# A two-layer attention trunk in fp32: where tables, inputs, gates and fetched outputs have their places, and in which order the last projection runs

## The chip, the cores and the metric

The kernel runs on one core of a Trainium2 chip. The metric is the device time of one execution in microseconds (us); the median over several executions counts. The engines are TensorE (PE in the profile; its weight loads, PEld, run beside its matmuls), VectorE (DVE), ScalarE (ACT), GpSimd (POOL) and SyncE (SP), which issues all DMAs of this kernel. Each engine takes its instructions in order.

## The reference, cut to what matters

The input is x, 2048 tokens by 1024 channels. Two layers follow each other, each with a residual sum:

```python
# layer 0
h = rms_norm(x, norm_g)
aq, ak, av, ag, bq, bk, bv, bg = split(h @ w_in)
aq, ak = rope(rms_norm(aq)), rope(rms_norm(ak))      # 8 query heads, 2 key heads of 64
ya = sliding_window_sink_attention(aq, ak, av, sinks) * silu(ag)
yb = chunked_relbias_attention(rms_norm(bq), rms_norm(bk), bv, rel) * silu(bg)
x = x + concatenate([ya, yb]) @ w_out
# layer 1
h = rms_norm(x, norm_g)
q, k, v, gate = split(h @ w_in)                      # 8 heads of 2 x 64, values of 128
q1, q2, k1, k2 = rope(rms_norm(...))
a = softmax(mask(q1 k1)) - lam * softmax(mask(q2 k2))
o = rms_norm(a @ v, subln_g) * (1 - lambda_init)
x = x + (o * silu(gate)) @ w_out
```

The sink is one more entry of each softmax row, so the row's maximum is also taken with it. Rope needs tables of cos and sin, multiplied by the norm's gains.

## The kernel before

All matmuls of projections and scores are in fp32 accuracy: operands are split into a high and a low part (names ending in H and L, made by a copy on ScalarE and a subtraction on VectorE or GpSimd), and `mm3` (L214 to L216) issues three matmuls for each product.

Tokens are in four blocks of 512. The kernel has four stages: layer 0's projection (names p0, to about 605 us), its attention with output projection (m, to about 1190), layer 1's projection (p1, to 1776) and layer 1's attention with gates and output projection (c, to the end). Layer 0's projection writes queries, keys, values and gates to DRAM, but leaves its last eight gate tiles to the next stage: `late_gate` there computes them between attention heads, on tiles of `yp`'s ring "xr", which has two slots (L783, L784). Layer 0's output tiles (`out_tile`, L495 to L505) take an x tile by DMA, accumulate in PSUM, add (L504) and store.

Layer 0's attention A takes the row maximum of two query tiles at once (L635) and then the minimum with the negated sink (L636, 128x2), which the exponential on ScalarE (L640) needs.

Each projection fetches cos and sin into the ring "xt" of its pool `xp` (three tiles, L267 to L270), which x tiles use too, and `rope_tables` (L185 to L193) builds two pairs of tables on VectorE: eight products of 128x512 and three scalings in each layer. In layer 1 the tables come first in the program. `weights` (L302 to L310) loads two weight tiles per DMA and splits them, the low part on GpSimd; with `first` set, every other low part goes to VectorE. The first two blocks' hidden tiles are then made from x: norm (L324, L326), transposes (L331), high and low part (L335, L336).

Layer 1's attention loops over heads and query blocks: scores (L913, L914), their maximum (L917) and exponential (L920), then transposes (L959) and products with values (L966), a norm by a matmul with ones (L991) and the gate. In blocks but the first the head's output is stored to DRAM, and `fetch` (L1016 to L1021) brings it back as "oy" and splits it at once on ScalarE (L1012) and GpSimd (L1013), for the output projection, which runs between the heads (`projected`, and `projected_last` for the last block: column half 1 in four PSUM tiles at a time, then half 0). "oy", the x tiles and the gates share ring "ot" of four.

Which work stands in which order is settled when the kernel is built: the program yields work in units that `pace` mixes, and a list scheduler with a simulated timeline then orders each engine's instructions; buffers of a ring are taken in program order. The pools of a stage are laid one behind another in the order in which they are opened. The first use of a pool waits for all users of every older pool on whose storage it lies. In layer 1's attention the pool `ld`, which holds queries, is opened third and lies over the projection's weight tiles (`wp`) and x tiles. `issue_after` puts an instruction behind another in its engine's order without a semaphore of its own.

Of the kernel before, what the change touches and what calls it, by code (L numbers as in the profile page):

```python
# [10 lines left out]
F32 = mybir.dt.float32  # L11
# [74 lines left out]
class Trunk:  # L86
# [137 lines left out]
    def _project(self, es, layer):  # L224
# [39 lines left out]
        def tables():  # L264
            if layer == 0:
                self.parameters(xp.tile([P, D], F32, tag="xt", name=n + "tmp"))
            self.cos = xp.tile([P, S // P, 32], F32, tag="xt", name=n + "cos")  # L267
            self.sin = xp.tile([P, S // P, 32], F32, tag="xt", name=n + "sin")
            nc.sync.dma_start(self.cos, a["cos"].rearrange("(t p) d -> p t d", p=P))
            nc.sync.dma_start(self.sin, a["sin"].rearrange("(t p) d -> p t d", p=P))  # L270
            gq, gk = ("ev_a_q_norm", "ev_a_k_norm") if layer == 0 else ("od_q_norm", "od_k_norm")
            tabs["q"] = self.rope_tables(tb, self.gain[gq], 0.125, n + "tq")
            tabs["k"] = self.rope_tables(tb, self.gain[gk], 1.0, n + "tk")
# [145 lines left out]
        for half in range(2):  # L419
# [13 lines left out]
            for gi, (kind, c0, width, o) in enumerate(groups):  # L433
                w = ready or weights(c0, width)
# [54 lines left out]
    def out_tile(self, y, w, j, t, c, xin, xout, sb, pmm, n, tag, xtag="xr", xbufs=None, order=range(KT), after=None):  # L489
# [14 lines left out]
        nc.vector.tensor_tensor(xr, ps, xr, ALU.add)  # L504
# [18 lines left out]
    def _mix0(self, es):  # L523
# [71 lines left out]
        def join(yt, O, e):  # L595
            hi = slice(e * HD, (e + 1) * HD)
            lo = slice((1 - e) * HD, (2 - e) * HD)
            tmp = sb.tile([P, BLK], F32, tag="low", name=n + "low")
            nc.scalar.activation(tmp[hi, :], O[lo, :], AF.Copy)
            nc.vector.tensor_tensor(yt[hi, :], O[hi, :], tmp[hi, :], ALU.add)  # L600
# [14 lines left out]
        def scores_a(h, b, res):  # L615
# [7 lines left out]
            for z in range(2):  # L623
# [12 lines left out]
                nc.vector.tensor_scalar(nm[:, zs], nm[:, zs], self.nsink[:, h:h + 1], None, ALU.min)  # L636
# [117 lines left out]
        def projected(b):  # L754
# [11 lines left out]
            for j, c in units:  # L766
                while next_load(c):
                    pass
                pm, tag = (pO, "O") if b == 0 and j % 2 else (pmm, "om")
                after = follow if b and (j, c) == units[-1] else None  # L770
                yield from self.out_tile(
                    split[b], w, j, b * NTB + j, c, a["x"], self.x1, yp, pm, n, tag, xbufs=2, order=ended, after=after
                )

        def late_gate(b, c, wg, h, r0):
# [7 lines left out]
            sg = yp.tile([P, BLK], F32, tag="xr", name=n + "sg", bufs=2)  # L783
# [73 lines left out]
    def _mix1(self, es):  # L857
        nc, tc, a, s = self.nc, self.tc, self.a, self.s1
        n = "c"
        pool = lambda nm, bufs, **kw: es.enter_context(tc.tile_pool(name=n + nm, bufs=bufs, **kw))  # L860
        ot = pool("ot", 4)
        sm = pool("sm", 8)
        ld = pool("ld", 2)
        yp = pool("y", 2 * KT)
        vp = pool("v", 4)
        pp = pool("pp", 20)
# [25 lines left out]
        def scores(h, b, q, K, res, then):  # L892
# [4 lines left out]
            for j in range(NTB):  # L897
# [9 lines left out]
                for m in range(2):  # L907
                    chunks = []
                    for z, (c, ce) in enumerate(cuts):
# [10 lines left out]
                        nc.scalar.activation(chunks[z][:, :wd], ps, AF.Exp, bias=nm[:, m, z:z + 1], accum_out=acc)  # L920
# [94 lines left out]

        def fetch(h, b):  # L1016

            if (h, b) in ended and h not in y[b]:
                o = ot.tile([P, BLK], F32, tag="ot", name=n + "oy")
                nc.sync.dma_start(o, s["o"][h * P:(h + 1) * P, b * BLK:(b + 1) * BLK])  # L1020
                split(h, b, o)  # L1021
# [53 lines left out]
        def out_begin(b, j, c):  # L1075
# [3 lines left out]
            pl, tag = (pG, "G") if b < NB - 1 else (pS, "S")  # L1079
# [11 lines left out]
        def projected(b):  # L1091
# [3 lines left out]
            for i, c in enumerate(halves):  # L1095
                for j in range(NTB):
                    xr, ps, to = out_begin(b, j, c)
                    for k in range(KT):
                        out_step(b, j, k, ps, w)
                        if j == NTB - 1 and i == 0:  # L1100
                            load_w(halves[1], k, w[k])
                        elif j == NTB - 1:
                            fetch(k, b + 1)
# [4 lines left out]
        def projected_last():  # L1108
# [15 lines left out]
            for c, w in ((1, w[0]), (0, pairs)):  # L1124
                tiles = [out_begin(b, j, c) for j in range(NTB)]
                for k in range(KT):
                    while (k, b) not in ended:
                        yield 0
                    for j in range(NTB):
                        out_step(b, j, k, tiles[j][1], w)  # L1130
                    yield 1
                for t in tiles:
                    out_end(*t)
# [45 lines left out]
        def side():  # L1179
            yield from gates()  # L1180
            for b in range(NB):
                for h in range(8):
                    while (h, b) not in ended and b < NB - 1:
                        yield 0
                    fetch(h, b)
# [50 lines left out]
```

## Time and profile before

| | us |
|---|---|
| median of 3 runs | 2843.03 (2841.9 to 2843.21) |
| the profiled execution | 2843.39 |
| its span in the trace | 2841.6 |
| TensorE busy | 2707.3 (95%) |
| VectorE busy | 1844.8 (65%) |
| GpSimd busy | 1596.6 (56%) |
| ScalarE busy | 1543.8 (54%) |

All rows below are of the profiled execution; their times count from the start of its span. In a timeline a row has start, length, engine, line, operation, result and operands, shape and count, and in brackets the idle time of the engine ahead of it and what ended that. In a table of windows a row has the stretch, its length, the busy time (and number of instructions) of TensorE, its weight loads, VectorE, ScalarE and GpSimd, the clock granted to TensorE as a share of full speed, the DMA engines' busy share and the GB/s moved. Waits are given as total us, number of times and longest.

### The profile page before, as it was taken

Reading aid. Unit: us, or ns where it says so; the run is one execution under the profiler, and the core shown is the slowest. Engines: PE = TensorE matmul, PEld = TensorE weight load, DVE = VectorE, ACT = ScalarE, POOL = GpSimd, SP = SyncE. Lnnn points to the kernel's source line nnn. Section 1 sums busy time; section 2 is a strip of 40 time slices with the busy share of each in tenths; the row PEclk is TensorE's granted clock in tenths of the full one; section 3 lists DMA queues with packets and bytes.
Section 4 is the critical chain, followed back from the end, with each engine's and each line's share of the span. In section 5 each row is a group of like instructions: output and inputs, shape, how many; then the busy total and the mean of one; then the engine's idle time right before and its main releaser. Section 6 shows DMA issues by size and latency. Waiting matters only on the chain.

```text
span 2841.6 us, 43911 instructions
## 1 busy us (share of the span) xinstructions
PE 2707.3 (95%) x13384; PEld 2171.4 (76%) x13384; DVE 1844.8 (65%) x4643; ACT 1543.8 (54%) x4015; POOL 1596.6 (56%) x1740
## 2 busy tenths in 40 slices
PE   7999999999899999899999999899999999999998
PEld 5888888887788888777788888777676777676766
DVE  7752285347788886498808870468787777666651
ACT  4443543367766666243334331468787676666751
POOL 3541252234545454267745560468888887888871
PEclk9999999999999999999999999999999999999999
DMA  5674343738887765476885443887868676464542
GB/s 161 228 233 149 108 140 120 220 117 232 218 197 186 190 181 150 155 271 198 254 255 189 141 126 108 251 251 212 248 187 232 180 212 207 120 191 131 176 137 81
DMA packets 356092, 521.68 MB, mean 184 GB/s; under 512 B 44816, under 2 KB 139792, under 8 KB 355856
## 3 DMA queue, kind: packets, MB, share of 16 engines
q1 hardware_dynamic: 355856, 518.87, 61.6%
q8 instruction: 107, 1.75, 0.3%
q14 instruction: 129, 1.06, 0.1%
HBM read 361.70 MB, written 157.02 MB: 183 GB/s over the span
## 4 chain that ended last, share of the span: by engine, by line
PE 73%; DVE 9%; DMA 9%; ACT 4%; issue 2%; POOL 2%; SPq 1%; DVEq 0%; ACTq 0%; POOLq 0%
PE cO L966 7%; PE p1mm L214 5%; PE p1mm L216 5%; PE p1mm L215 5%; PE cS L913 4%; PE cS L914 4%; PE ctr L959 3%; PE p0mm L214 3%; PE p0mm L216 3%; PE p0mm L215 3%; PE com L214 2%; PE com L215 2%; PE com L216 2%; PE mom L214 2%; PE cG L214 2%
## 5 line engine op out<-in xcount | busy, mean ns | idle before, releaser
L920 ACT ACTIVATE cP<-cS,cnm 128x512 f32<-128x512 f32 (+3 forms) x640 | 397.3, 628 | 181.6 <-DVE cnm L917 142.9
L917 DVE TENSOR_REDUCE cnm<-cS 128x1 f32<-128x512 f32 (+3 forms) x640 | 371.7, 601 | 80.0 <-PE cS L914 74.1
L936 POOL TENSOR_SCALAR cP<-cP,crl,ce 128x512 f32<-128x512 f32 (+3 forms) x288 | 220.0, 778 | 164.2 <-DVE crl L931 84.7
L215 PE MATMUL p1mm<-p1wL,p1hH 128*128 128x512 f32 x768 | 302.3, 394 | 0.4 <-POOL p1wL L310 0.4
L214 PE MATMUL p1mm<-p1wH,p1hH 128*128 128x512 f32 x768 | 301.1, 393 | 0.8 <-ACT p1wH L308 0.8
L216 PE MATMUL p1mm<-p1wH,p1hL 128*128 128x512 f32 x768 | 301.8, 393 | 0.0
L310 POOL TENSOR_TENSOR p0wL<-p0ws,p0wH 128x512 fp32r<-128x512 f32 (+1 forms) x124 | 149.4, 1237 | 266.8 <-ACT p0wH L308 257.8
L966 PE MATMUL cO<-cpt,cv 128*128 128x512 f32 (+3 forms) x640 | 287.7, 537 | 4.2 <-DVE cpt L964 3.6
L946 POOL TENSOR_TENSOR cP<-cP,cP 128x512 f32<-128x512 f32 (+3 forms) x256 | 285.5, 1140 | 1.4
L913 PE MATMUL cS<-ck,cqd 128*128 128x512 f32 (+3 forms) x640 | 261.2, 413 | 12.4 <-ACT cP L920 7.1
L214 PE MATMUL p0mm<-p0wH,p0hH 128*128 128x512 f32 (+1 forms) x640 | 239.9, 377 | 5.2 <-ACT p0vt L472 3.5
L310 POOL TENSOR_TENSOR p1wL<-p1ws,p1wH 128x512 fp32r<-128x512 f32 x128 | 169.2, 1342 | 133.6 <-ACT p1wH L308 126.4
L216 PE MATMUL p0mm<-p0wH,p0hL 128*128 128x512 f32 (+1 forms) x640 | 239.6, 375 | 1.8 <-DVE p0hL L336 1.8
L215 PE MATMUL p0mm<-p0wL,p0hH 128*128 128x512 f32 (+1 forms) x640 | 239.2, 374 | 0.0
L914 PE MATMUL cS<-ck,cql 128*128 128x512 f32 (+3 forms) x640 | 231.4, 367 | 4.4 <-DMA cql<-qL 4.4
L959 PEld LDWEIGHTS ctr<-ident,cP 128*128 128x128 f32 x1088 | 136.8, 141 | 109.7 <-issue 60.8
L945 POOL TENSOR_SCALAR cP<-cP,crl,ce 128x512 f32<-128x512 f32 (+3 forms) x230 | 180.0, 795 | 0.0
L959 PE MATMUL ctr<-ident,cP 128*128 128x128 f32 x1088 | 172.9, 274 | 0.8 <-ACT cpt L962 0.3
L214 PEld LDWEIGHTS p1mm<-p1wH,p1hH 128*128 128x128 f32 x768 | 144.7, 188 | 29.8 <-ACT p1wH L308 1.0
L215 PEld LDWEIGHTS p1mm<-p1wL,p1hH 128*128 128x128 f32 x768 | 144.7, 188 | 29.5 <-POOL p1wL L310 0.8
L216 PEld LDWEIGHTS p1mm<-p1wH,p1hL 128*128 128x128 f32 x768 | 144.7, 188 | 28.8
L913 PEld LDWEIGHTS cS<-ck,cqd 128*128 128x128 f32 x640 | 121.9, 191 | 44.6 <-ACT cP L920 19.9
(306 smaller groups left out, 7271.1 us busy)
## 6 DMA issues: line engine op xcount, KB each, us to landing
p1ws<-in_od_w_in_dram SPq DMA_DIRECT2D x56, 512.0 KB, 4.4
p0ws<-in_ev_w_in_dram SPq DMA_DIRECT2D x48, 512.0 KB, 4.4
ck<-kH SPq DMA_DIRECT2D x144, 128.0 KB, 3.3
ck<-kL SPq DMA_DIRECT2D x144, 128.0 KB, 3.5
cv<-v SPq DMA_DIRECT2D x72, 256.0 KB, 4.5
cqd<-qH SPq DMA_DIRECT2D x128, 128.0 KB, 4.6
cql<-qL SPq DMA_DIRECT2D x128, 128.0 KB, 4.6
cwH<-wgH SPq DMA_DIRECT2D x64, 256.0 KB, 4.6
```

The lines of the kernel that those rows point to most:

```text
L214: mm(ps, aH, bH, start=first, stop=False)
L215: mm(ps, aH, bL, start=False, stop=False)
L216: mm(ps, aL, bH, start=False, stop=last)
L310: low.tensor_tensor(l[:, :width], ws[:, k, :width], f32(h[:, :width]), ALU.subtract)
L913: mm(ps, qd[:, m, js], kt[:, :wd], start=True, stop=False)
L914: self.anchor = mm(ps, ql[:, m, js], kt[:, :wd], start=False, stop=True).ins
L917: nc.vector.tensor_reduce(nm[:, m, z:z + 1], ps, AX.X, ALU.max, negate=True)
L920: nc.scalar.activation(chunks[z][:, :wd], ps, AF.Exp, bias=nm[:, m, z:z + 1], accum_out=acc)
L936: nc.gpsimd.tensor_scalar(p1, p1, rl[:, 0:1], e1, ALU.mult, ALU.mult)
L946: nc.gpsimd.tensor_tensor(p1, p1, p2, ALU.add)
L959: nc.tensor.transpose(tp[:, (j - j0) * P:(j - j0 + 1) * P], us[j][kt // 4][:, kk:kk + P], self.ident)
L966: mm(O[:, j0 * P:], v, T[:, :wd], start=(kt == 0), stop=(kt == nkt - 1), skip_group_check=True)
```

## The change

Seven edits:

1. cos and sin go into ring "xn" of pool `sb` (5 tiles) in both layers, and layer 1's tables are ordered behind the last sum of layer 0 (`self.added`). The first weights of layer 1 take their odd low parts on VectorE (`first`).
2. "low" in layer 0's attention has one buffer instead of two, and "sg" of the late gates a buffer of its own in that pool.
3. The sink minimum is two operations of 128x1.
4. For layer 0's last output block the even x tiles come from pool `yt`.
5. Layer 1's attention opens `ld` first, then `sm` and `ot`; "P0" has 19 buffers instead of 20.
6. Fetched outputs have a ring "oy" of two; their split is issued one fetch later (or ahead of the next projection), behind the newest exponential in ScalarE's order.
7. `projected_last` accumulates half 1 to the last head but one, then one tile of half 0 (`ahead`, in the bank of the gates), then the last head for both, and the other tiles of half 0 one by one.

```diff
--- before.py
+++ after.py
@@ -264,13 +264,14 @@
                 self.parameters(xp.tile([P, D], F32, tag="xt", name=n + "tmp"))
-            self.cos = xp.tile([P, S // P, 32], F32, tag="xt", name=n + "cos")
-            self.sin = xp.tile([P, S // P, 32], F32, tag="xt", name=n + "sin")
+            self.cos = sb.tile([P, S // P, 32], F32, tag="xn", name=n + "cos", bufs=5)
+            self.sin = sb.tile([P, S // P, 32], F32, tag="xn", name=n + "sin", bufs=5)
             nc.sync.dma_start(self.cos, a["cos"].rearrange("(t p) d -> p t d", p=P))
...
             gq, gk = ("ev_a_q_norm", "ev_a_k_norm") if layer == 0 else ("od_q_norm", "od_k_norm")
-            tabs["q"] = self.rope_tables(tb, self.gain[gq], 0.125, n + "tq")
-            tabs["k"] = self.rope_tables(tb, self.gain[gk], 1.0, n + "tk")
+            with self.tc.issue_after(self.added) if layer else nullcontext():
+                tabs["q"] = self.rope_tables(tb, self.gain[gq], 0.125, n + "tq")
+                tabs["k"] = self.rope_tables(tb, self.gain[gk], 1.0, n + "tk")
@@ -431,7 +432,7 @@
             for gi, (kind, c0, width, o) in enumerate(groups):
-                w = ready or weights(c0, width)
+                w = ready or weights(c0, width, first=half == gi == 0)
                 ready = None
@@ -501,7 +502,7 @@
             yield 1
-        nc.vector.tensor_tensor(xr, ps, xr, ALU.add)
+        self.added = nc.vector.tensor_tensor(xr, ps, xr, ALU.add).ins
         nc.sync.dma_start(xout[tok, cs], xr)
@@ -595,7 +596,7 @@
             lo = slice((1 - e) * HD, (2 - e) * HD)
-            tmp = sb.tile([P, BLK], F32, tag="low", name=n + "low")
+            tmp = sb.tile([P, BLK], F32, tag="low", name=n + "low", bufs=1)
             nc.scalar.activation(tmp[hi, :], O[lo, :], AF.Copy)
@@ -633,7 +634,8 @@
                 nc.vector.tensor_reduce(nm[:, zs], ps, AX.X, ALU.max, negate=True)
-                nc.vector.tensor_scalar(nm[:, zs], nm[:, zs], self.nsink[:, h:h + 1], None, ALU.min)
+                for j in (2 * z, 2 * z + 1):
+                    nc.vector.tensor_scalar(nm[:, j:j + 1], nm[:, j:j + 1], self.nsink[:, h:h + 1], None, ALU.min)
                 yield 1
@@ -767,9 +769,10 @@
                 pm, tag = (pO, "O") if b == 0 and j % 2 else (pmm, "om")
+                xp, xt, xb = (yp, "xr", 2) if b or j % 2 else (self.yt, "yt", None)
                 after = follow if b and (j, c) == units[-1] else None
                 yield from self.out_tile(
-                    split[b], w, j, b * NTB + j, c, a["x"], self.x1, yp, pm, n, tag, xbufs=2, order=ended, after=after
+                    split[b], w, j, b * NTB + j, c, a["x"], self.x1, xp, pm, n, tag, xtag=xt, xbufs=xb, order=ended, after=after
                 )
@@ -780,7 +783,7 @@
                 yield 1
-            sg = yp.tile([P, BLK], F32, tag="xr", name=n + "sg", bufs=2)
+            sg = sb.tile([P, BLK], F32, tag="sg", name=n + "sg", bufs=1)
             gt = yp.tile([P, BLK], F32, tag="xr", name=n + "gt", bufs=2)
@@ -858,12 +861,12 @@
         pool = lambda nm, bufs, **kw: es.enter_context(tc.tile_pool(name=n + nm, bufs=bufs, **kw))
+        ld = pool("ld", 2)
+        sm = pool("sm", 8)
         ot = pool("ot", 4)
-        sm = pool("sm", 8)
-        ld = pool("ld", 2)
         yp = pool("y", 2 * KT)
         vp = pool("v", 4)
-        pp = pool("pp", 20)
+        pp = pool("pp", 19)
         kp = pool("kp", 4)
@@ -917,7 +920,9 @@
                         acc = la[:, m, z:z + 1] if nb > 1 else l[:, m:m + 1]
-                        nc.scalar.activation(chunks[z][:, :wd], ps, AF.Exp, bias=nm[:, m, z:z + 1], accum_out=acc)
+                        self.exp = nc.scalar.activation(
+                            chunks[z][:, :wd], ps, AF.Exp, bias=nm[:, m, z:z + 1], accum_out=acc
+                        ).ins
                         then(j, m, z)
@@ -1013,12 +1018,19 @@
+        fetched = []
+
         def fetch(h, b):
...
             if (h, b) in ended and h not in y[b]:
-                o = ot.tile([P, BLK], F32, tag="ot", name=n + "oy")
+                o = ot.tile([P, BLK], F32, tag="oy", name=n + "oy", bufs=2)
                 nc.sync.dma_start(o, s["o"][h * P:(h + 1) * P, b * BLK:(b + 1) * BLK])
-                split(h, b, o)
+                fetched.append((h, b, o))
+
+        def split_fetched(left):
+            if len(fetched) > left:
+                with tc.issue_after(self.exp):
+                    split(*fetched.pop(0))
@@ -1072,11 +1084,13 @@
-        def out_begin(b, j, c):
+        def out_begin(b, j, c, pl=None, tag="S"):
             rows, cols = slice((b * NTB + j) * P, (b * NTB + j + 1) * P), slice(c * 512, (c + 1) * 512)
...
             nc.sync.dma_start(xr, self.x1[rows, cols])
-            pl, tag = (pG, "G") if b < NB - 1 else (pS, "S")
+            if b < NB - 1:
+                pl, tag = pG, "G"
+            pl = pl or pS
             return xr, pl.tile([P, 512], F32, tag=tag, name=n + "om"), self.out[rows, cols]
@@ -1096,10 +1110,13 @@
                     for k in range(KT):
+                        if i == j == 0:
+                            split_fetched(0)
                         out_step(b, j, k, ps, w)
...
                         elif j == NTB - 1:
+                            split_fetched(1)
                             fetch(k, b + 1)
@@ -1121,16 +1138,29 @@
                 load_w(0, k, pairs[k])
-            for c, w in ((1, w[0]), (0, pairs)):
-                tiles = [out_begin(b, j, c) for j in range(NTB)]
+            def step(js, tiles, w, k):
+                while (k, b) not in ended:
+                    yield 0
+                for j, t in zip(js, tiles):
+                    out_step(b, j, k, t[1], w)
+                yield 1
+
+            first = [out_begin(b, j, 1) for j in range(NTB)]
+            for k in range(KT - 1):
+                yield from step(range(NTB), first, w[0], k)
+            ahead = [out_begin(b, 0, 0, pG, "G")]
+            for k in range(KT - 1):
+                yield from step((0,), ahead, pairs, k)
+            yield from step(range(NTB), first, w[0], KT - 1)
+            for t in first:
+                out_end(*t)
+            yield from step((0,), ahead, pairs, KT - 1)
+            out_end(*ahead[0])
+            for j in range(1, NTB):
+                t = out_begin(b, j, 0)
                 for k in range(KT):
-                    while (k, b) not in ended:
-                        yield 0
-                    for j in range(NTB):
-                        out_step(b, j, k, tiles[j][1], w)
-                    yield 1
-                for t in tiles:
-                    out_end(*t)
+                    yield from step((j,), (t,), pairs, k)
+                out_end(*t)
@@ -1180,9 +1210,13 @@
                 for h in range(8):
-                    while (h, b) not in ended and b < NB - 1:
+                    while (h, b) not in ended and (h, b) not in place:
                         yield 0
-                    fetch(h, b)
+                    if all(f[:2] != (h, b) for f in fetched):
+                        fetch(h, b)
+                if b == NB - 1:
+                    while fetched:
+                        split_fetched(0)
                 yield from projected(b) if b < NB - 1 else projected_last()
```

## Rows read from the trace of the kernel before

**Rows 1.** The page's part 1, the span of 2841.6 us.
```profile
PE 2707.3 (95%) x13384; PEld 2171.4 (76%) x13384; DVE 1844.8 (65%) x4643; ACT 1543.8 (54%) x4015; POOL 1596.6 (56%) x1740
```

**Rows 2.** Windows: length, busy PE, PEld, DVE, ACT, POOL, granted clock, DMA share, GB/s.
```profile
36.00:57.00 21.00, 14.72 (x58) 11.16 (x58) 20.37 (x57) 10.97 (x29) 8.52 (x6) 0.84 0.34 114
600.00:1140.00 540.00, 502.51 (x3104) 440.07 (x3102) 418.52 (x1465) 373.60 (x992) 261.76 (x390) 0.98 0.73 188
700.00:712.00 12.00, 7.60 (x28) 5.80 (x27) 4.25 (x14) 6.76 (x16) 7.05 (x13) 0.72 0.79 188
737.00:746.00 9.00, 5.00 (x27) 4.41 (x26) 7.37 (x14) 5.41 (x15) 7.54 (x13) 0.81 0.70 171
1148.00:1160.00 12.00, 5.97 (x18) 4.46 (x17) 9.99 (x25) 4.74 (x11) 0.00 (x0) 0.72 0.87 273
1190.00:1400.00 210.00, 195.62 (x925) 158.38 (x924) 191.01 (x322) 93.95 (x223) 147.88 (x113) 0.99 0.70 234
1400.00:1776.00 376.00, 376.00 (x1762) 312.12 (x1760) 189.73 (x352) 127.53 (x277) 186.63 (x144) 1.00 0.54 170
1776.00:1792.00 16.00, 7.37 (x26) 6.02 (x25) 3.90 (x18) 3.77 (x13) 1.89 (x5) 0.68 0.76 190
2804.00:2816.00 12.00, 6.90 (x21) 4.21 (x20) 2.61 (x5) 3.29 (x6) 2.54 (x2) 0.86 0.07 22
```

**Rows 3.** The chain that ended last, 1150 to 1165, in order of time.
```profile
1154.87 0.79 PE mom L214
...
1159.04 0.23 PE mom L214
```

**Rows 4.** Timeline of VectorE: start, length, [idle before it <- what ended it].
```profile
31.26 0.69 DVE L185 TENSOR_TENSOR p0tqC<-p0cos,ev_a_q_norm 128x512 f32<-128x512 f32 x1 [1.20 <-DMA p0cos<-in_cos_dram]
```

**Rows 5.** Timeline of ScalarE and TensorE behind a late gate.
```profile
702.57 0.63 ACT L786 ACTIVATE msg<-mgt 128x512 f32<-128x512 f32 x1 [2.02 <-DMA g<-mgt]
...
704.47 0.44 PE L739 MATMUL mtrB<-ident,mPB 128*128 128x128 f32 x2 [3.50 <-DVE mptL L592]
```

**Rows 6.** Line 636, the sink minimum: durations in ns, and who waited.
```profile
L636 DVE TENSOR_SCALAR manm<-manm,nsink x64: 149/221/4312, 607.3 to 1096.4; 128x2 f32<-128x2 f32 x64
...
  ACT mPA L640: 20.4, 18
```

**Rows 7.** Timeline of VectorE, GpSimd and TensorE around the longest minimum.
```profile
734.75 2.56 POOL L612 TENSOR_TENSOR myL<-myt,myH 128x512 fp32r<-128x512 f32 x2
...
735.48 4.31 DVE L636 TENSOR_SCALAR manm<-manm,nsink 128x2 f32<-128x2 f32 x1
...
738.46 1.30 POOL L612 TENSOR_TENSOR myL<-myt,myH 128x512 fp32r<-128x512 f32 x1
...
741.45 0.41 PE L739 MATMUL mtrB<-ident,mPB 128*128 128x128 f32 x2 [3.75 <-DVE mptL L592]
```

**Rows 8.** Line 932, a 128x1 operation of VectorE.
```profile
L932 DVE TENSOR_SCALAR crl<-crl,nlam x128: 136/214/218, 1790.0 to 2760.1; 128x1 f32<-128x1 f32 x128
```

**Rows 9.** Timeline of VectorE at the layer boundary.
```profile
1148.59 0.69 DVE L185 TENSOR_TENSOR p1tqC<-p1cos,od_q_norm 128x512 f32<-128x512 f32 x1 [6.22 <-DMA p1cos<-in_cos_dram]
```

**Rows 10.** Waits of TensorE over the span: us, times, longest.
```profile
PE p1trq L384 <- DVE p1eL L390: 7.4, 6, 2.9
...
PE com L214 <- ACT cy L1012: 3.1, 2, 2.7
```

**Rows 11.** Line 207 in layer 1's projection, 1190 to 1776.
```profile
L207 DVE TENSOR_TENSOR p1q8u<-p1q8u,p1q8ms x64: 153/1148/1286, 1217.2 to 1692.1; 128x8 f32<-128x8 f32 x64
```

**Rows 12.** Waits of SP's queue over the span.
```profile
SPq L888 <- PE p1mm L216: 4.4, 1, 4.4
```

**Rows 13.** Timeline of TensorE at the start of layer 1's attention.
```profile
1785.19 0.45 PE L914 MATMUL cS<-ck,cql 128*128 128x128 f32 x1 [4.39 <-DMA cql<-qL]
```

**Rows 14.** What the instructions on the fetched outputs' tiles waited for.
```profile
  DMA coy<-o: 16.5, 6
```

**Rows 15.** Timeline of TensorE in the tail.
```profile
2811.41 0.79 PE L214 MATMUL com<-p1hH,cyk 128*128 128x512 f32 x1 [3.67 <-ACT cyk L1012]
```

## The prediction

> **What bounds the kernel now.** I read the busy times first. TensorE has 2707.3 us of work in a span of 2841.6 us [rows 1], so it is the bound, and 134.3 us of idle time, with the matmuls that ran at the lower clock, are all that a change of order can win. Then the stretches around each edit, in the table of windows [rows 2]: for each one the reader sees how much of it TensorE was idle and what clock was granted. Last come the chain, the waits and the timelines of those stretches, for what ended each idle time.
>
> I price every stretch alike. Idle time is its length less TensorE's busy time; the clock takes at most (1 - granted clock) x length, and less, since part of the low level falls into the idle time itself. At the layer boundary the chain shows what part: nine matmuls from 1154.87 to 1159.04, the first at 0.79, then the step falls to 0.23 us, the 2.4 GHz level [rows 3]. That is 4.17 us where 9 x 0.23 = 2.07 would do: 2.1 of a possible 0.28 x 12.00 = 3.36, so 0.6 of it. I use 0.6 throughout. From [rows 2], idle plus 0.6 of the clock:
> start 36 to 57: 6.28 + 2.0 = 8.3; late gate 700 to 712: 4.40 + 2.0 = 6.4; sink minimum 737 to 746: 4.00 + 1.0 = 5.0; layer boundary 1148 to 1160: 6.03 + 2.0 = 8.0; queries 1776 to 1792: 8.63 + 3.1 = 11.7; tail 2804 to 2816: 5.10 + 1.0 = 6.1. Together 45.5 us, which the change can at most take out of these six.
>
> **The start.** Layer 0's cos and sin leave the ring of three "xt" tiles, so their transfers no longer wait for a slot and the next x block no longer waits for them. But VectorE is busy for 20.37 of the 21 us [rows 2], with the tables among its work: an earlier transfer removes none of that work, only waits such as the 1.20 us ahead of the first table operation [rows 4]. Lower bound 0, upper the 8.3 of the stretch. As VectorE is nearly full, the truth is nearest to the row of 1.20, with a share of the clock: I take 2.
>
> **The late gate.** The gate's exponential waits 2.02 us for the store that still holds its slot of the two-slot ring, and TensorE then 3.50 for work behind it [rows 5]. With "sg" in a place of its own that wait has no cause. The "low" ring that loses a buffer is used once per pair of heads; its next user waits only if the pairs finish closer together than one add. I take 6 of 6.4 (4 to 6.4, since another wait may lie 2 us behind). The x loads of layer 0's output that move to "yt" were not late in these stretches: nothing; if that cover is gone, one such load is late by the 2.02 us of [rows 5], which lies in the bounds.
>
> **The sink minimum.** The 64 minima of 128x2 have a median of 221 ns but go up to 4312, and ScalarE waited 20.4 us for them [rows 6]. The longest runs from 735.48 to 739.79, while GpSimd works without a break from 734.75 to 739.76, and TensorE then idles 3.75 [rows 7]. A 128x1 operation of the same kind, with a scalar from SBUF, took at most 218 ns in 128 cases [rows 8]. So the 4.31 becomes about 0.4, and the stretch gives 5.0. The Trainium skill, page "SBUF — State Buffer", section "Who interferes with whom", says why: VectorE and GpSimd share a port pair as an exclusive lock, and a VectorE operation with two SBUF inputs, or a tensor_scalar in its two-port mode, is blocked for the whole of the other's instruction. The rows agree with it as far as GpSimd is busy throughout the 4.31 us; that 128x1 escapes the lock is shown by [rows 8] alone. The price: 64 more operations at 0.15 to 0.22 us, 10 to 14 us of VectorE, against 540 - 418.5 = 121.5 idle there [rows 2]; about 1 us may land on the path. Net 4 (0, if other GpSimd pairs block what follows instead, to 9, if the other 16 ScalarE waits also reached TensorE).
>
> **The layer boundary.** VectorE waits 6.22 us for layer 1's cos, whose slot lies in storage that layer 0 still used, and then works through the tables ahead of layer 0's pending sums [rows 9]; TensorE, which needs the banks that those sums free, idles for 6.03 us of the twelve [rows 2]. With the tables held until after the last sum of layer 0, all 8.0 go. But the work comes back at about 1190. The tables are eleven operations, at most 0.69 us each in the row shown; nine of them stand between 1148.59 and the restart of TensorE at 1154.87 with the sum that it waits for, so 0.6 each: 11 x 0.6 = 6.6 us. The first weights' odd low parts also move from GpSimd to VectorE: four of 0.69, 2.8 us. That is 9.4 us more on VectorE, whose first job there is the first two hidden blocks. From 1190 to 1400 it is busy 191.01 of 210 us and TensorE idles 14.4 [rows 2]; TensorE's largest wait there is for VectorE [rows 10]. VectorE has 19 us of idle time in those 210, but the 9.4 come in the first 25, so I let about half of them fit: 5 given back (1, nearly all hidden, to 10, all on the path). From 1400 TensorE is busy without a gap [rows 2], so what is lost there stays lost. Net 3 (-2 to 7).
>
> The tables will run beside GpSimd's low parts, as they did not before. What that can do is shown by a small operation of layer 1 with two inputs in SBUF: 153 ns at best, 1148 in the middle, 1286 at worst [rows 11]. Were each of the 15 moved operations delayed by the difference of some 1.1 to 1.3 us, 15 x 1.3 = 19.5 would come on top of the 9.4; this is a rival below (C2).
> The port rule of the Trainium skill, same page and section, speaks against this part of the change: table operations and low parts read two SBUF tensors each, so they and GpSimd's operations would exclude one another. By it the boundary would cost, by the row's own figures, 29 instead of 5; [rows 11] agrees in size.
>
> **Layer 1's queries.** Layer 1's projection ends at about 1776, and the first query transfer waits 4.4 us for its last matmul [rows 12], because the pool that holds queries lies over the projection's weight tiles. TensorE then idles until the query parts land, 4.39 us before 1785.19 alone [rows 13]. Opened first, that pool lies over the 32 KB of the projection's hidden block, whose last reader comes four tiles of 24 matmuls ahead of the end, 96 x 0.23 = 22 us [rows 3]. The transfers then land before the last matmul. What is left is the queue: SP must come to them in order, behind value stores that wait for their evictions, and the score banks must be free. Of 11.7 I take 10 (7, if the store after the last matmul must still drain before the first exponential can go on, to 11.7).
>
> **Fetched outputs.** The transfers get a ring of two, and their split moves one fetch later and behind the newest exponential. Now ScalarE sits idle for them 16.5 us in 6 cases [rows 14], and TensorE waits only for a part, 3.1 us in two cases [rows 10]. I take 2.5 (0, if the ring of two makes the loads late instead, to 6, with ScalarE's lateness counted where it delays exponentials). One score buffer less (20 to 19) is hidden by the same ring's depth: nothing.
>
> **The tail.** TensorE idles 5.10 us of the twelve [rows 2], 3.67 of them at once, for the last head's output [rows 15]. The new order has one more tile of the second half, 7 x 3 matmuls of 0.23, 4.8 us, that doesn't need that head. It fills the gaps if it is still undone at 2804. I take 4.5 of 6.1 (0, if the order built beforehand spends this tile earlier).
>
> **New waits.** The order on all engines is planned anew; small waits, 134.3 less the 34.4 of the six stretches, 100 us in all, will move. I take 4 us lost (from 4 won to 12 lost).
>
> **Sum.** 2 + 6 + 4 + 3 + 10 + 2.5 + 4.5 = 32, less 4: 28. The profiled execution took 2843.39 us, 1.8 more than its span and 0.36 above the median. 2843.4 - 28 = 2815.4; I say 2815.
>
> **Rivals.** *A, the sum:* 2815, with 2803 to 2826 for itself (its terms off by about 12 together).
> *B, only the two waits with one clear cause go*, late gate and queries, 16, less the 4: 2831; with the boundary's 3, 2828. For it: VectorE is full at the start and after 1190; the tail's tile may be used early. Against it: the minimum and the boundary have as plain a cause. I say 2829.
> *C, nothing shows:* the queries' transfers stay behind SP's value stores, and stalls of the same size appear elsewhere: 2838 to 2843. The rows speak for SP being late elsewhere, but not for a full exchange.
> *C2, the moved work is delayed by GpSimd:* 9.4 + 19.5 = 28.9 given back instead of 5: 32 - 4 - 24 = 4 won, 2839, within 0.2%. For it: [rows 11]. Against it: it needs GpSimd busy beside every one of the operations, and GpSimd is busy for 147.88 of the 210 us [rows 2], waits for its weights first, and loses four operations itself. (This is the outcome by the Trainium skill's "Who interferes with whom".)
> *D, slower:* the same place, but each of the 15 operations delayed by two GpSimd operations in turn, 2.6 us: 39 + 9.4 = 48 given back, 28 + 5 - 48 = -15: 2858. It decides from 33 + 5.7 = 39 us given back. Blocks of 4.31 us exist [rows 7], fifteen in a row do not.
>
> **Chances.** A 0.62, B 0.21, C 0.08, C2 0.05, D 0.04. Some 0.2% (5.7 us) is what a measurement of this kernel can tell from no change. Faster is A and B, 0.83; same is C and C2, 0.13; slower D, 0.04. All lower ends together win 4 + 7 - 2 - 12 and so nothing; all upper ones 8.3 + 6.4 + 9 + 7 + 11.7 + 6 + 6.1 + 4 = 58.5, 2785. Neither is likely as a whole. The range is 2798 (A with 17 more won over all its terms) to 2834 (5 past B): it leaves out C, C2 and D, 0.17, and some 0.03 at the low end.
>
> **What would show it.** Right: the first query transfer is issued about 20 us ahead of the last projection matmul and TensorE's idle time after that is under 2 us; no wait for layer 1's cos ahead of layer 0's sums, and the tables behind the last of them; VectorE's minima at most 0.25 us; no gate exponential waiting for a store; output matmuls between the last norm matmuls and the last head's output. Wrong: TensorE's idle time in the 200 us after the layer boundary grows by 10 or more; the tail's gap stays at 3.7; ScalarE's waits for fetched outputs stay at 16; new waits of 3 us and more in the second layer's attention.

## The result, and the profile after

The changed kernel is slower: median 2845.14 us of 22 runs (2836.63 to 2852.74) against 2839.38 of 22 (2827.63 to 2847.37) for the kernel before, a ratio of 1.0024 with a 95% interval of 1.0014 to 1.0035. The forecast was 2815. Its profiled execution has a span of 2848.3 us, 6.7 more than before. Single executions of one kernel spread over some 20 us here, so the verdicts below go by ratios over several runs with their 95% intervals, and the traces are read for where they differ.

The busy time, part 1 of the page of after:

```profile
PE 2711.3 (95%) x13384; PEld 2178.1 (76%) x13384; DVE 1844.3 (65%) x4711; ACT 1543.5 (54%) x4015; POOL 1583.3 (56%) x1736
```

TensorE has the same 13384 matmuls. Its idle time is 2.7 us longer, and the other 4.0 us are busy time: the mean granted clock is 0.984, before it was 0.987. The table of windows of after shows the stretches of [rows 2] at the place they have now:

```profile
34.00:55.00 21.00, 19.18 (x98) 15.20 (x96) 20.60 (x59) 12.00 (x33) 8.73 (x6) 1.00 0.29 86
697.00:709.00 12.00, 10.21 (x58) 8.32 (x57) 9.02 (x34) 8.54 (x22) 6.48 (x13) 1.00 0.77 178
720.00:740.00 20.00, 14.45 (x88) 11.69 (x87) 13.01 (x40) 15.16 (x42) 16.86 (x22) 0.92 0.84 181
1134.00:1146.00 12.00, 9.88 (x37) 7.72 (x36) 5.28 (x16) 4.84 (x12) 0.47 (x1) 0.86 1.07 291
1174.00:1384.00 210.00, 192.68 (x901) 156.43 (x900) 188.36 (x326) 91.23 (x214) 141.68 (x106) 0.98 0.69 229
1764.00:1780.00 16.00, 15.55 (x76) 12.78 (x75) 7.01 (x28) 7.39 (x24) 7.13 (x12) 1.00 0.74 234
2815.00:2827.00 12.00, 6.99 (x22) 4.45 (x21) 2.00 (x4) 3.55 (x6) 2.54 (x2) 0.86 0.07 22
```

Read them against the old ones. Start, late gate and queries are fuller now and at full clock (the queries: 15.55 of 16 us, 7.37 before). The layer boundary has 2.1 us of idle time left of 6.03, the stretch behind it idles more (17.3 of 210, 14.4 before), and the tail is as it was.

The summaries of three tiles in after give the last matmul of each stage (count, shortest, median and longest in ns, start of the first and of the last):

```profile
L216 PE MATMUL mom<-mw,myL x256: 387/393/794, 755.0 to 1173.8; 128*128 128x512 f32 x128
```

```profile
L216 PE MATMUL p1mm<-p1wH,p1hL x768: 387/389/776, 1182.6 to 1766.0; 128*128 128x512 f32 x192
```

```profile
L917 PE MATMUL cS<-ck,cql x640: 272/389/632, 1766.3 to 2764.9; 128*128 128x512 f32 x136, 128*128 128x128 f32 x8, 128*128 128x384 f32 x8, 128*128 128x256 f32 x8
```

And the same three of before:

```profile
L216 PE MATMUL mom<-mw,myL x256: 388/393/628, 765.6 to 1189.3; 128*128 128x512 f32 x128
```

```profile
L216 PE MATMUL p1mm<-p1wH,p1hL x768: 387/389/628, 1195.2 to 1775.9; 128*128 128x512 f32 x192
```

```profile
L914 PE MATMUL cS<-ck,cql x640: 272/390/628, 1785.2 to 2756.3; 128*128 128x512 f32 x136, 128*128 128x256 f32 x9, 128*128 128x128 f32 x8, 128*128 128x384 f32 x7
```

So the kernel is 15.5 us ahead at the end of layer 0, 9.9 ahead at the end of layer 1's projection, some 21 once the queries' wait is past too (11 more, below), and 8.6 behind at the last score. Everything that was won is lost in layer 1's attention, and more. TensorE's longest waits in that stage of after:

```profile
PE cS L916 <- ACT cP L923: 22.0, 26, 3.0
...
PE cG L214 <- DMA cwH<-wgH: 11.2, 3, 5.5
...
PE com L214 <- ACT cyk L1017: 3.7, 1, 3.7
```

Score matmuls wait 22.0 us, in 26 cases, for a PSUM bank that an exponential still reads; before it was 7.1 us in 11. The second line grew too: gate matmuls waited 4.2 us for their weights before, 11.2 now.

### The profile page after: what moved, and what is told of

Its sections match the earlier page's. It is cut to its first block, busy times and chain, and to the rows that moved or that the text cites. A ratio compares the mean times of both kernels' runs of the same rounds, so it can differ in the third digit from the quotient of the medians.

```text
span 2848.3 us, 43994 instructions
## 1 busy us (share of the span) xinstructions
PE 2711.3 (95%) x13384; PEld 2178.1 (76%) x13384; DVE 1844.3 (65%) x4711; ACT 1543.5 (54%) x4015; POOL 1583.3 (56%) x1736
## 4 chain that ended last, share of the span: by engine, by line
PE 71%; DVE 11%; DMA 8%; ACT 5%; issue 2%; POOL 2%; SPq 1%; DVEq 0%; ACTq 0%; POOLq 0%
PE cO L971 7%; PE p1mm L215 5%; PE p1mm L216 5%; PE p1mm L214 5%; PE cS L916 4%; PE cS L917 3%; PE ctr L964 3%; PE p0mm L214 3%; PE p0mm L216 3%; PE p0mm L215 3%; PE com L214 2%; PE com L215 2%; PE mom L214 2%; PE com L216 2%; PE mom L216 2%
## 5 line engine op out<-in xcount | busy, mean ns | idle before, releaser
L941 POOL TENSOR_SCALAR cP<-cP,crl,ce 128x512 f32<-128x512 f32 (+3 forms) x288 | 219.0, 773 | 194.8 <-DVE crl L936 67.4
L950 POOL TENSOR_SCALAR cP<-cP,crl,ce 128x512 f32<-128x512 f32 (+3 forms) x230 | 174.5, 769 | 0.0
```

The lines of the kernel that those rows point to most:

```text
L941: nc.gpsimd.tensor_scalar(p1, p1, rl[:, 0:1], e1, ALU.mult, ALU.mult)
```

## The experiments

Both traces leave three theories: **F**, the fetched outputs' edit (6) costs; **Q**, the queries' new pool order (5) spoils the order of the stage; **P**, the twentieth buffer of the score ring "P0" (it holds exponentials), given up in edit 5, costs. Edits 1 to 4 lie ahead of that stage; every variant keeps them but e5, which is the kernel before, and e12, which leaves out a part of edit 1. In the expectations "the first kernel" is e1, and in that of e16 "the kernel before" is e15.

**Which edit.** Four kernels with edits 1 to 4 and these further edits (in e1 and e3 the ring keeps its 20):

```diff
# e1_queries: edit 5 without its buffer     # e2_queries_19: edit 5
-        pp = pool("pp", 19)
+        pp = pool("pp", 20)
# e3_no_fetch: e1 and edit 7                # e4_no_tail: e2 and edit 6
```

Expected of e1: 

> Edits 1 to 5 with 20 score buffers kept; fetched outputs (edit 6) and tail (edit 7) as before. Theory F (the fetched outputs' edit costs the second layer's attention some 28 us): this kernel keeps the some 20 us that the profile of after had won by 1814, so a ratio near 0.993. Rival Q (opening the queries' pool first spoils the planned order of the second layer's attention): the wins are lost here too, ratio 1.00 or more. Rival R (any new plan of that stage is about as slow, the plan of before was a lucky one): 0.998 to 1.002.

Expected of e2: 

> As the first kernel of this call, but with 19 score buffers instead of 20. Theory F: within 0.1% of the first kernel, near 0.993. Rival P (the buffer taken from the score ring is what costs): some 20 us slower than the first, ratio near 1.00, and the waits of score matmuls for exponentials near 20 us, as after.

Expected of e3: 

> After without edit 6: edits 1 to 5 and 7, with 20 score buffers. Theory F: as the first kernel or up to 5 us faster (the tail), ratio 0.991 to 0.993. Rival Q: 1.00 or more. If the tail's edit costs: slower than the first kernel.

Expected of e4: 

> After without edit 7: edits 1 to 6. Theory F and rivals P and Q alike: as after, ratio 1.000 to 1.003, since in after the tail stood as before. If edit 7 costs: faster than after by more than 0.2%.

Measured ratios to before: e1 0.9955 (0.9941 to 0.9969), e2 1.0035 (1.0019 to 1.0051), e3 0.9951 (0.9934 to 0.9968), e4 1.0022 (1.0005 to 1.0038). Between e1 and e2 there is one number in one line, and 23.5 us in the medians (2826.85, 2850.39). F and Q are out as the main cause, as is rival R, that any new plan is about as slow; P stands. The tail's edit is worth nothing (e3 beside e1, after beside e4). TensorE's waits of e1 and then of e2:

```profile
PE cS L916 <- ACT cP L923: 6.1, 11, 1.3
```

```profile
PE cS L916 <- ACT cP L923: 24.3, 26, 2.7
```

**How the buffers' number acts.**

```diff
# e5_before_19, on the kernel before
-        pp = pool("pp", 20)
+        pp = pool("pp", 19)
# e6_queries_18 and e7_queries_21, on e1: 18 and 21
# e8_all_20, on after: 20, and for the room
-        sm = pool("sm", 8)
+        sm = pool("sm", 6)
```

Expected of e5: 

> The kernel before with 19 score buffers instead of 20 and nothing else. Theory P (the twentieth buffer is worth some 23 us in the second layer's attention): ratio 1.006 to 1.010, TensorE's waits of score matmuls for exponentials from 7.1 to 20 us or more. Rival S (the loss came from how 19 buffers met the queries' new pool order, not from 19 as such): 0.998 to 1.002.

Expected of e6: 

> Edits 1 to 5 with 18 score buffers (fetched outputs and tail as before). Theory P: at least as slow as with 19, ratio 1.003 to 1.012. Rival L (each number of buffers gives another planned order, and 19 drew a bad one): anywhere from 0.995 on, no order in the numbers.

Expected of e7: 

> Edits 1 to 5 with 21 score buffers. Theory P with a step at 20 (a row of the last block is four tiles, and five rows fit into 20): as with 20, 0.994 to 0.997. Theory P without a step (the more the better): 0.988 to 0.992. Rival L: may be slower than with 20 by 10 us.

Expected of e8: 

> All seven edits, but 20 score buffers; the 448 bytes that are missing for it come from the pool of small tiles (six of each instead of eight). Theory P: 0.991 to 0.996, some 20 us faster than after. If the fetched outputs' edit costs by itself, or six small tiles are too few: 0.997 or more.

Measured: e5 1.0081 (1.0061 to 1.0102), e6 1.0069 (1.0052 to 1.0086), e7 0.9964 (0.9949 to 0.9978), e8 0.9997 (0.998 to 1.0014). The number alone costs 23 us on the kernel before too, with waits as in after:

```profile
PE cS L913 <- ACT cP L920: 21.1, 25, 3.8
```

A twenty-first buffer brings nothing: a step at 20. From 18 to 20 the ratios fall with the number, which speaks against rival L. Two readings need care. The total of these waits is no price by itself: e7, with no loss, has 12.7 us of them. And the number of buffers also changes the plan: e1's and e2's traces have the same matmuls, but from the 10317th of 13384 on, in the block before the last, their order on TensorE differs. What e2 and e5 price is a buffer together with the plan that is made for it.

But e8, all edits with 20 buffers, came out higher than expected; either six small tiles or the fetched outputs cost.

**Small tiles, room from elsewhere, a shorter lead, the boundary.**

```diff
# e9_small_6, on e1
-        sm = pool("sm", 8)
+        sm = pool("sm", 6)
# e10_all_20_ot3, on after with 20 buffers
-        ot = pool("ot", 4)
+        ot = pool("ot", 3)
# e11_19_lag_32, on e2
-    BANKS1, LAG1 = (4, 2, 1, 1), (30, 30, 36, 36)
+    BANKS1, LAG1 = (4, 2, 1, 1), (30, 30, 32, 32)
# e12_no_boundary, on e1
-            with self.tc.issue_after(self.added) if layer else nullcontext():
+            with nullcontext():
-                w = ready or weights(c0, width, first=half == gi == 0)
+                w = ready or weights(c0, width)
```

Expected of e9: 

> Edits 1 to 5 with 20 score buffers and six small tiles instead of eight; every engine's planned order is that of the first kernel of the study. If the six small tiles cost what the kernel with all edits and 20 buffers lost: ratio 0.999 to 1.001. If they cost nothing (then the fetched outputs' edit costs 10 us by itself): 0.994 to 0.997.

Expected of e10: 

> All seven edits with 20 score buffers, the place taken from ring ot (three instead of four). If the fetched outputs' edit costs by itself: 0.998 to 1.002, as with six small tiles. If not: 0.992 to 0.996.

Expected of e11: 

> Edits 1 to 5 with 19 score buffers, and in the last two blocks the program lets scores run ahead of values by 32 units of 128 columns instead of 36 (one buffer holds four). Theory W (the program's order asks for a lead that 19 buffers can't hold, so that exponentials come late): most of the loss comes back, ratio 0.995 to 0.999. Rival (the loss is that scores have less lead over values, whatever the program asks): no gain over 19 buffers with 36, 1.002 to 1.006, or worse.

Expected of e12: 

> Edits 1 to 5 with 20 score buffers, but layer 1's tables ahead of layer 0's last sums again, and its first low parts on GpSimd again (their inputs keep the new place). The lag read from the traces says that the boundary won 4 and gave back 6: then within 0.2% of the first kernel, 0.994 to 0.997. If the prediction's sum held (8 won, 5 given back): 0.997 to 0.999.

Measured: e9 0.9945 (0.9924 to 0.9967), six small tiles cost nothing, so by its expectation edits 6 and 7 make e8 slower than e9, by 0.5%. e10 0.9975 (0.996 to 0.9991), between the two cases; TensorE runs the same order of matmuls as in e8 throughout, so the 0.2% between them, with intervals that overlap, need not be ring "ot". e11 1.0016 (1.0002 to 1.003): asking for less lead brings back at most some 0.2% of the 0.8% between 19 and 20, with intervals that overlap; theory W wanted most of it. e12 0.9964 (0.9948 to 0.998): the order of the tables and the low parts on VectorE are worth nothing that can be seen, but the interval reaches from the one case into the other.

**Theory ROW.** By the code, in the last block each of a head's four query tiles has four chunks of columns, 16 buffers, which are held until the head's transposes have read them. The next head's first query tile needs four more: 16 + 4 = 20. In the block before, a head has 12. The last chunk of a head's first query tile has only 128 columns, in a buffer for 512. So give these chunks tiles of their own:

```diff
# e13_19_small, on e2; e15_all_19_small, on after
+                        if wd == P and not m:
+                            chunks.append(pp.tile([P, P], F32, tag="P0s", name=n + "P0s", bufs=2))
+                        else:
...
# e14_16, on e2
-        pp = pool("pp", 19)
+        pp = pool("pp", 16)
# e16_split_free, on e15
-                with tc.issue_after(self.exp):
-                    split(*fetched.pop(0))
+                split(*fetched.pop(0))
```

Expected of e13: 

> Edits 1 to 5 with 19 score buffers, but each head's one chunk of 128 columns per softmax goes to two small tiles of its own (1 KB in all) instead of a full buffer. A head of the last block then holds 15 full buffers and has four left for the next head's first row, as with 20. Theory ROW (the next head's first row of four chunks must find a place while the head before it still holds its own): the loss is gone, ratio 0.994 to 0.997. Rival N (the number of full buffers counts): as with 19, 1.002 to 1.006.

Expected of e14: 

> Edits 1 to 5 with 16 score buffers: no room at all for the next head's first row in the last block (16 chunks a head), and four left in the block before it (12 a head). Theory ROW: the loss falls in the last block and is larger than with 18 or 19 (1.0035 and 1.0069), ratio 1.010 or more, its TensorE waits for score banks there over 16 us; the first three blocks lose less than 5 us. Rival (any number under 20 gives another planned order with a loss of the same size): 1.003 to 1.007.

Expected of e15: 

> All seven edits with 19 score buffers and the small tiles for the chunks of 128 columns; eight small tiles of softmax sums and four of ring ot, as in after. Theory ROW: 0.994 to 0.999, some 15 us faster than after; if the fetched outputs' edit costs some 5 to 10 us by itself, the upper half of that range. Rival N: as after, 1.001 to 1.004.

Expected of e16: 

> As the kernel before in this call, but the split of a fetched output is not ordered behind the newest exponential. If that order is what the fetched outputs' edit costs: faster than the kernel before by 0.2 to 0.4%. If the later split or the ring of two costs: no difference beyond 0.2%.

Measured: e13 0.995 (0.9935 to 0.9965), e14 1.0221 (1.0208 to 1.0235), e15 0.996 (0.9948 to 0.9972), e16 0.9981 (0.9968 to 0.9995). One kilobyte per partition in the right place gives back what the buffer had cost: rival N is out, and ROW's forecasts of the times held for e13, e14 and e15. The windows from the first to the last score of the last block say where (for after, e1 and e14 the block ahead of it comes first). Before, after, e1 (20) and e2 (19):

```profile
2357.00:2756.00 399.00, 386.75 (x1716) 277.84 (x1715) 269.90 (x610) 261.24 (x717) 329.64 (x359) 0.98 0.52 157
```

```profile
2066.00:2352.00 286.00, 278.52 (x1259) 203.15 (x1258) 215.97 (x508) 203.07 (x579) 230.82 (x262) 0.98 0.68 198
2352.00:2765.00 413.00, 390.97 (x1728) 281.41 (x1727) 282.61 (x613) 263.17 (x723) 323.15 (x357) 0.98 0.51 153
```

```profile
2062.00:2343.00 281.00, 275.37 (x1256) 200.84 (x1255) 218.02 (x507) 202.77 (x577) 228.42 (x258) 0.99 0.69 201
2343.00:2739.00 396.00, 385.35 (x1719) 277.88 (x1718) 271.93 (x609) 261.12 (x719) 329.71 (x360) 0.99 0.52 158
```

```profile
2352.00:2768.00 416.00, 393.80 (x1724) 282.88 (x1723) 284.97 (x612) 262.43 (x720) 321.97 (x357) 0.97 0.50 151
```

And e6 (18), e14 (16), e13 (19 with small tiles), e15 (all edits, 19 with small tiles):

```profile
2346.00:2770.00 424.00, 397.30 (x1728) 283.20 (x1727) 280.45 (x614) 261.65 (x720) 324.40 (x356) 0.96 0.51 149
```

```profile
2066.00:2360.00 294.00, 281.61 (x1267) 203.85 (x1266) 214.82 (x509) 204.37 (x580) 225.21 (x260) 0.98 0.66 192
2360.00:2820.00 460.00, 402.50 (x1729) 286.30 (x1728) 277.79 (x612) 262.76 (x721) 320.87 (x356) 0.93 0.47 138
```

```profile
2337.00:2729.00 392.00, 383.00 (x1717) 276.34 (x1716) 289.73 (x613) 257.80 (x721) 327.36 (x357) 0.99 0.54 160
```

```profile
2344.00:2738.00 394.00, 381.78 (x1722) 276.00 (x1719) 284.79 (x614) 260.11 (x721) 327.61 (x358) 1.00 0.54 160
```

The second number is the last block's length: 392 to 399 us in these runs where the first row finds its place, 413 to 424 with 18 or 19 buffers, 460 with 16. Runs not shown fit less well: e3, e8 and e10, with 20, took 400 to 402 us, e11, with 19 and less lead, 410, and e16, with e15's ring, 409. Of the 20 us between e1 and e2 in this block 11.6 are idle time of TensorE and 8.4 longer busy time, at a granted clock of 0.97 against 0.99.

ROW is not the whole of it. In the block ahead, where 12 buffers of a head and three for the next first row fit into 16, it forecasts no loss, and e14's expectation wanted less than 5 us in the first three blocks; yet this block is 5 us longer than in e1 with 19 buffers (after) and 13 with 16. And score matmuls of e14's last block wait 2.3 us for exponentials, not the expected 16. With 16 there is nothing of the next head to work on while GpSimd still scales and sums the current one, and TensorE waits there instead, where e1 has 0.3:

```profile
PE ctr L962 <- POOL cP L949: 30.6, 5, 9.4
```

As for the split: without its place behind the exponential e16 is 0.2% slower than e15, with intervals that overlap a little; there is no sign that the order costs.

## Why the prediction was wrong

The step that failed is the last sentence under "Fetched outputs": "One score buffer less (20 to 19) is hidden by the same ring's depth: nothing." It is worth some 23 us by e1 and e2, 23 by e5, and some 18 by after and e15, which gets by without it. The depth was never counted against what must lie in the ring at once, which the code gives (16 of the head in work, four of the next one's first tile); 20 was exactly enough. The term "new waits", 4 us with 12 at worst, could not hold it.

The forecast change was 28 us down and the measured one 5.8 up, so more than the buffer is missing: e15, with all seven edits and no loss in the ring, wins 0.4%, some 11 us. The other terms together were too high, as the table below shows. And the base was too high: the forecast took its 28 us off an execution of 2843.4, which lies 4 us above the median of the 22 runs.

Slower was forecast by rival D alone, and for a wrong reason. No table operation was held up, as VectorE's timeline of after shows (the last three of the eight products), though GpSimd began two low parts beside them. These took 4.61 us where the line's mean is 1.35 each, so the delay fell on GpSimd:

```profile
1177.84 0.69 DVE L186 TENSOR_TENSOR p1tkC<-p1cos,od_k_norm 128x512 f32<-128x512 f32 x1
1178.45 0.69 DVE L187 TENSOR_TENSOR p1tkS<-p1sin,od_k_norm 128x512 f32<-128x512 f32 x1
1179.05 0.69 DVE L188 TENSOR_TENSOR p1tkS<-p1sin,od_k_norm 128x512 f32<-128x512 f32 x1
```

```profile
1178.06 4.61 POOL L311 TENSOR_TENSOR p1wL<-p1ws,p1wH 128x512 fp32r<-128x512 f32 x2 [43.59 <-ACT p1wH L309]
```

The other terms, by the ends of the stages in the two traces:

| term | forecast | found in the traces |
|---|---|---|
| start | 2 (0 to 8.3) | 5.2: the last gate matmul of the first stage at 599.5, before 604.7 |
| gate, minimum, boundary's removal | 6 + 4 + 8 = 18 | 10.3: 15.5 at the end of layer 0, less the 5.2; 4.6 and 4.9 of it by the windows of gate and boundary |
| given back by the boundary | 5 | 5.6: 15.5 shrinks to 9.9 by the projection's end, but not shown to be the boundary's |
| queries | 10 | 11: idle time and clock 11.7 before, 0.45 now |
| fetched outputs | 2.5 | no gain seen (e13 beside e15); e8 beside e9 is 0.5% slower |
| tail | 4.5 | not seen (e3 beside e1) |
| new waits | -4 (4 to -12) | for gate weights alone 11.2 us against 4.2; 4.8 to 12.0 in all variants with the new pool order, 4.7 in e5 |

**Start.** More than taken: VectorE is as full as before, but TensorE now has work beside it (19.18 of 21 us). In the other traces with edit 1 this stage ends at 598.0 to 601.9, so 2.8 to 6.7 us were won.

**Gate, minimum, boundary.** The gate's stretch went from 6.4 lost to 1.8. With the 4.9 won at the boundary, that leaves 0.8 us of the 10.3 for the minimum, where 4 was forecast. The minima are short now, the first line below (its summary in after), yet ScalarE waits for them nearly as long, the second: 18.2 us against 20.4 [rows 6]. By the timelines a minimum was at work during only 7.5 of the 20.4 us, and during 2.3 of the 18.2: the rest of the wait was never the minimum's own. The stretch around the old stall idles 5.55 of 20 us in after (720 to 740, above) and idled 4.48 of 20 before, the last line: other waits took the stall's place.

```profile
L638 DVE TENSOR_SCALAR manm<-manm,nsink x128: 141/199/216, 602.1 to 1085.0; 128x1 f32<-128x1 f32 x128
...
  ACT mPA L642: 18.2, 13
```

```profile
727.00:747.00 20.00, 15.52 (x93) 13.62 (x92) 15.56 (x36) 14.90 (x40) 17.92 (x24) 0.91 0.73 164
```

At the boundary 2.1 us of idle time and 1.0 of clock are left, so 4.9 of 8.0 were won. But they did not need the tables' new order: e12 leaves that order out, and of edit 1 it keeps only the new place of cos and sin. TensorE's restart there comes after the same gap, the first line for after and the second for e12. The new place is the likely cause; it was not tested apart from edits 2 to 4:

```profile
1139.66 0.79 PE L214 MATMUL mom<-mw,myH 128*128 128x512 f32 x1 [2.12 <-DVE mxr L505]
```

```profile
1139.26 0.50 PE L214 MATMUL mom<-mw,myH 128*128 128x512 f32 x1 [2.04 <-DVE mxr L505]
```

Nor is the tables' work on VectorE shown to be what is given back: from the last output matmul of layer 0 to the last of layer 1's projection before took 586.6 us, after 592.2, e1 593.9 and e12, whose tables run early, 596.0. The net of 3 us can't be told from nothing by e1 and e12 (0.9955 and 0.9964).

**Queries.** Right in place and size: the first transfer is issued 21 us ahead of the last projection matmul, by SP's timeline of after, and the first score follows that matmul at once, by TensorE's:

```profile
1744.63 0.45 SPq L891 DMA_DIRECT2D cqd<-qH  x1
```

```profile
1766.19 0.22 PE L916 MATMUL cS<-ck,cqd 128*128 128x128 f32 x1
```

**Fetched outputs.** ScalarE's engine waits for them as long as before, 17.3 us in 6 cases against 16.5 [rows 14], now with exponentials right behind; TensorE's wait for the splits fell from 3.1 [rows 10] to 0.2.

The sign "ScalarE's waits for fetched outputs stay at 16" was among those that the prediction gave for being wrong, and it came.

**Tail.** The rival condition came true, "0, if the order built beforehand spends this tile earlier": the tile's matmuls on the first seven heads were over at 2804.9. The gap of [rows 15] is there to the hundredth:

```profile
2822.71 0.79 PE L214 MATMUL com<-p1hH,cyk 128*128 128x512 f32 x1 [3.67 <-ACT cyk L1017]
```

Left open: why 18 buffers are slower than 19, when neither holds a full row, and why the block ahead of the last loses too; how much of a buffer's price is the shorter ring and how much the plan made for it; and where the some 10 us come from that e8 and e10 lie above e1, e9 and e15. In their traces half of these lie in the last block. The other half lies in the first two, which took 299.6 and 299.8 us there and 294.0 in e1; but after and e4, with the same order of matmuls in these two blocks, took 300.1 and 293.9, so that half may be spread.

## What to carry to other kernels

Before a ring gives up a buffer, count what it must hold at one time in the stage where rows are longest, not how deep it looks: the price here was nothing from 21 to 20, 23 us from 20 to 19, and 2.7% of the time from 20 to 16. Where a planner reads the ring's size, the price is that of another plan as well. Where room is short, look for the small chunk in a full-size buffer: two tiles of 512 bytes per partition did what a buffer of 2 KB did, and with them all seven edits are 0.4% faster than the kernel before. A wait that is removed is only won when the stage behind it can use the time, so check a change by the time at which each stage ends, and its parts one at a time: here the gain that the prediction had put down to an order was there without it.

## What was not expected of the hardware

A VectorE operation with two operands in SBUF can wait through several GpSimd operations in a row, not one. In after's last block a combination that takes 0.99 us at the median took 5.63, and four score maxima ran right behind it. The rows in VectorE's timeline, and GpSimd's beside them:

```profile
2562.22 5.63 DVE L948 SCALAR_TENSOR_TENSOR cP<-cP,cc,cP 128x512 f32<-128x512 f32 x1
2567.78 2.07 DVE L920 TENSOR_REDUCE cnm<-cS 128x1 f32<-128x512 f32 x4
```

```profile
2560.07 2.26 POOL L950 TENSOR_SCALAR cP<-cP,crl,ce 128x512 f32<-128x512 f32 x3
2562.30 1.29 POOL L992 TENSOR_TENSOR cot<-cot,cgg 128x512 f32<-128x512 f32 x1
2563.55 3.76 POOL L951 TENSOR_TENSOR cP<-cP,cP 128x512 f32<-128x512 f32 x3
```

It begins while GpSimd is still in the last of the first three, and ends 0.5 us after the last of four more. The Trainium skill, page "SBUF — State Buffer", section "Who interferes with whom", says that the side that comes second is blocked until the first one's instruction is finished; the trace agrees that it is blocked, but here the wait did not end with one instruction. Such a wait does not explain the missing buffer's price: the longest of these combinations is 5.6 to 6.1 us in after, e2, e4 and e5, which have 19 buffers, and 1.48 in e1 and 1.59 in before, but it is 6.29 in e15, which has no loss, and 2.2 in e6 and e14, which lose more.
